# Splitting a weight block's cast from its low part, a second queue for the blocks, and float32r filter taps in a one-core encoder block

## The chip, the cores and the metric

The kernel runs on one core of one Trainium2 chip. The metric is the device time of one execution in microseconds (us). A run consists of several executions of the same program; the profile is one more execution, recorded by the hardware profiler. All tensors are float32 in DRAM.

## The reference, cut to what matters

One encoder block on 512 tokens of width 2048. What matters here is the beginning of it: the modulation, the first projection with the columns of `z_h`, and the filters of the long convolution, which depend on no token at all.

```
mod = silu(c) @ w_ada + b_ada            # c: (1, 2048), w_ada: (2048, 6*2048)
sh1, sc1, g1, sh2, sc2, g2 = split(mod)
h   = x * (1 + sc1) + sh1
z   = h @ w_in + b_in                    # w_in: (2048, 9216)
...
h   = sin(freq * (feats @ w1 + b1)); h = sin(freq * (h @ w2 + b2))
filt = (h @ w3) * window                 # the taps of the filters, then their transforms
...
x   = LN(alpha * x + g1 * mix)           # then an MLP with 2048 -> 8192 -> 2048
```

## The kernel before, in words

Every large product is done in three float32r matmuls, because a float32r operand keeps only part of a float32's digits: an operand `a` is split into a high part (a cast to float32r) and a low part (`a` minus its high part), and `hi*hi + hi*lo + lo*hi` is summed in PSUM. The function `split` (L74) issues the two halves of a splitting together: the cast on ScalarE (L76), the subtraction on VectorE (L77).

Weights come in blocks of 128 by 1024 (512 KB, two row groups of 512 columns). The class `Weights` (L113) keeps a ring of three raw blocks, three high and three low parts. `prepare` takes a loaded raw block, casts it, subtracts, and asks for the next load; all of its loads go out on SyncE's queue (SP). `take` hands the next ready block to a product. Blocks are used in the order of `blocks()`.

The program has four stretches.

**Head.** Small constants are loaded, `cond` (the vector c, the same in all partitions) is turned into silu(c), and the small network of the filters runs: two matmuls with a sine behind each (`Sine`, `Filters.middle`, `Filters.ready`).

**Filters.** Eight parts (n = 0 to 7, in `PARTS`). Each part has taps (four matmuls of the 64 hidden rows with a 512-column piece of w3, in plain float32, L387; every second part has one more for the skip row, L389), the product with a window on VectorE (L397), and a forward transform (`Forward`: six float32 matmuls, L321, L325, L333, and six VectorE sums). One pass of the loop issues the taps of part n+1, the transform of part n, two modulation chunks, the windowed product of part n+1, the stores of the part before, and the sums of part n.

**Value groups.** The modulation's first third (shift1, scale1) is a product of a row with a 2048 by 4096 matrix, and is done on VectorE: 64 chunks of 128 by 1024, each loaded (512 KB) and reduced against `cond` with one instruction (`Modulation.step`, L263). Four chunks give 128 columns of shift and scale; then `first_input` (L424) makes one row group of the activation `h1`: two small sums on GpSimd, two passes on ScalarE (L428, L429), one on GpSimd (L430). Twenty chunks are done during the filters and 44 are left here. Meanwhile two column groups of w_in (4 and 5, the values of the convolution) are computed side by side: `two` holds two generators of `dense_steps`, and each loop pass kp takes one block for each: 24 matmuls (L187) for a block, 16 blocks in all. Before the matmuls of a pass, `prepare` splits as many blocks as the ring holds, and then eight chunks are issued in one go (`ada_steps(4)` twice), so that `h1` is three row groups ahead (`LEAD`). Chunks wait in up to eight buffers of the activation's pool and three of their own, and the next one is asked for when one has been used; nine are on their way at a time while the pool has room. Each row group of `h1` that is finished takes one of these buffers.

**The rest.** All other projections, the convolutions, the branches, the output and the MLP, from the next column group of w_in (6) on.

Each engine runs its instructions in the order in which the code issues them, and so do the two queues' issuers: a DMA that waits holds back every DMA issued behind it on the same engine. Eight semaphores, in turn, serve all DMAs of SP and ScalarE, so that an issue also waits until an earlier DMA, about eight back, has landed.

Of the kernel before, what the change touches and what calls it, by code (L numbers as in the profile page):

```python
# [18 lines left out]
P = 128  # L19
# [21 lines left out]
def block_kernel(ctx: ExitStack, tc: tile.TileContext, t):  # L41
# [70 lines left out]
    class Weights:  # L112


        def __init__(self):
            self.blocks = blocks()
            self.raw, self.ready, self.kept, self.used = [], [], {}, set()
            self.ahead, self.done = 1, False

        def load(self):  # L120
# [5 lines left out]
            load(raw, w[cg, kp])  # L126
# [13 lines left out]
        def prepare(self):  # L140
            for _ in range(4):
# [5 lines left out]
                raw, what = self.raw.pop(0)  # L147
                hi, lo = self.tiles(what)
                split(raw, hi, lo)
                self.ready.append((hi, lo, what))  # L150
                self.load()

        def take(self, w, cg, kp):
            if (w.name, cg, kp) in self.used:
                return self.kept[w.name, cg, kp]
            if not self.done or self.raw:
                self.prepare()
# [67 lines left out]
    cond = const.tile([P, D], F32, name="cond")  # L225
    for h in range(4):
        c_ = slice(512 * h, 512 * (h + 1))
        load(cond[:, c_], t["c"][:, c_].broadcast_to([P, 512]))
# [9 lines left out]
    make_identity(nc, ident)  # L238

# [4 lines left out]
    class Modulation:  # L244
# [16 lines left out]
        def step(self):  # L261
# [3 lines left out]
            if len(self.raw) < 10:  # L265
                self.load()
# [80 lines left out]
    class Filters:  # L347


        def __init__(self):  # L350
            self.one = Sine(hw1, featT, 0, HID)
            self.src, self.raw, self.stores, self.kept, self.win, self.ps = [], [], [], {}, [], []
# [6 lines left out]
        def ready(self):  # L359

            x = self.two.reduce()
            even, odd = slot("a2"), slot("a2")
            nc.scalar.activation(even, x, AF.Sin)
            nc.scalar.activation(odd, x, AF.Sin, scale=sign)
            self.a2 = [a.rearrange("h (p k) -> h k p", k=4) for a in (even, odd)]
# [11 lines left out]

        def taps(self, n):

            cs = PARTS[n][2]  # L380
            if cs == 0:
                self.w = self.raw.pop(0)
            w, skip = self.w
            for cl in range(4):
                ps = bank("flt")
                extra = cs == 0 and cl == 0
                nc.tensor.matmul(ps, self.a2[cs][:, cl, :], w, start=True, stop=not extra)  # L387
# [70 lines left out]
    for s_, c_ in zip(silu, quarters):  # L458
        nc.scalar.activation(s_, c_, AF.Sigmoid)
    flt.middle()  # L460
# [23 lines left out]
    for m in (1, 4):  # L484
        nc.gpsimd.tensor_scalar(bada[:, m], bada[:, m], 1.0, None, op0=OP.add)
    ada_steps(2)
    flt.ready()
    x_load()
# [4 lines left out]
    flt.windowed(0)  # L493
    for n in range(8):
# [666 lines left out]
```

## Time and profile before

| | |
|---|---|
| runs of the kernel before | 2763.06, 2764.24, 2766.48 us (median 2764.24) |
| the profiled execution | 2763.92 us; span of its records 2762.1 us |
| mean granted TensorE clock | 0.993 |
| busy share of the span | TensorE 98%, VectorE 55%, ScalarE 28%, GpSimd 4% |
| bytes read from DRAM, written | 388.01 MB, 10.50 MB |
| head and first taps | 0 to 33.1 us |
| filters (parts 0 to 7) | 33.1 to 98.65 us |
| value groups | 98.65 to 212.6 us |
| the rest | 212.6 to 2762.1 us |

How to read it. PE is TensorE, PEld its weight loads, DVE VectorE, ACT ScalarE, POOL GpSimd, SP SyncE; SPq and ACTq are their DMA issues. Times are counted from the start of the span. The table by windows gives, for each stretch, its length, each engine's busy time with the number of instructions, the granted clock (1.00 is full speed), the mean busy share of the 16 DMA engines and the GB/s that they moved. The timeline gives start, duration, engine, line, operation, tiles, shapes and count, with the idle time before it and what ended that in brackets. A float32 matmul shows as two instructions, a float32r matmul as one. Busy times of neighbours overlap a little, so that the distance of two starts is the better measure of what one costs in a stream.

### The profile page before, as it was taken

To read this page: it belongs to the slowest core of one execution; us is meant where nothing else is said; L and a number is where in the kernel's file an instruction comes from. 1 tells how busy PE (TensorE), PEld (TensorE's weight loads), DVE (VectorE), ACT (ScalarE), POOL (GpSimd) and SP (SyncE) were. 2 spreads that over 40 slices of the span, in tenths; PEclk is the share of its full clock that TensorE was granted. 3 is DMA by queue.
4 is the path that set the end of the run, shared out by engine and by line. 5 is a ranking of instruction groups with operands and counts; after the bars stand their busy time and mean duration, and the time that the engine had idled before them with its cause. 6 is when DMAs were issued, how large, how long until landed. Compare 5 with 4: busy or idle time off the path is not lost.

```text
span 2762.1 us, 29764 instructions
## 1 busy us (share of the span) xinstructions
PE 2703.0 (98%) x11917; PEld 2199.8 (80%) x11917; DVE 1519.6 (55%) x2026; ACT 768.4 (28%) x932; POOL 109.3 (4%) x104
## 2 busy tenths in 40 slices
PE   7989999999999999999999999999999999999996
PEld 3667777888888888887988888888888888888885
DVE  7866968644566657546774343343433433434348
ACT  2234322322222222314631221312213122131232
POOL 1120000000000000050020000000000000000001
PEclk9989999999999999999999999999999999999998
DMA  8672332555665568454552222332222232223242
GB/s 321 241 293 82 127 102 99 190 193 191 201 207 191 185 202 287 139 185 163 167 163 96 99 92 101 98 99 94 97 99 94 97 99 98 94 92 107 93 143 77
DMA packets 120474, 400.46 MB, mean 145 GB/s; under 512 B 14219, under 2 KB 14315, under 8 KB 120208
## 3 DMA queue, kind: packets, MB, share of 16 engines
q1 hardware_dynamic: 119880, 398.20, 42.4%
q8 instruction: 93, 1.52, 0.2%
q10 hardware_dynamic: 456, 0.37, 0.0%
q14 instruction: 45, 0.37, 0.0%
HBM read 388.01 MB, written 10.50 MB: 144 GB/s over the span
## 4 chain that ended last, share of the span: by engine, by line
PE 88%; DVE 4%; DMA 1%; ACT 1%; issue 1%; POOL 0%; SPq 0%; DVEq 0%; ACTq 0%
PE d L187 56%; PE t L874 28%; PE inv L628 1%; DVE wlo L77 1%; PE inv L616 0%; DMA araw<-in_ada 0%; DMA wraw<-in_w_m 0%; DVE r L1026 0%; DVE r L890 0%; PE tr L539 0%; DVE r L1028 0%; PE h2T L914 0%; PE mix L750 0%; PE f L558 0%; PE f L556 0%
## 5 line engine op out<-in xcount | busy, mean ns | idle before, releaser
L187 PE MATMUL d<-act,whi 128*128 128x512 f32 (+1 forms) x4224 | 1285.1, 387 | 15.9 <-POOL act L430 9.0
L77 DVE TENSOR_TENSOR wlo<-wraw,whi 128x1024 fp32r<-128x1024 f32 x480 | 590.3, 1233 | 1030.7 <-ACT whi L76 1027.7
L76 ACT CAST whi<-wraw 128x1024 fp32r<-128x1024 f32 x480 | 504.5, 1054 | 1534.6 <-PE d L187 919.2
L187 PEld LDWEIGHTS d<-act,whi 128*128 128x128 f32 x4224 | 786.7, 189 | 181.3 <-POOL act L430 10.7
L187 PE MATMUL d<-act,wlo 128*128 128x512 f32 (+1 forms) x2112 | 811.9, 384 | 1.8 <-DVE wlo L77 1.8
L187 PEld LDWEIGHTS d<-act,wlo 128*128 128x128 f32 x2112 | 398.5, 189 | 81.7 <-DVE wlo L77 3.5
L874 PE MATMUL t<-whi,fh 128*128 128x512 f32 x960 | 373.4, 389 | 0.0
L874 PE MATMUL t<-wlo,fh 128*128 128x512 f32 x960 | 373.4, 389 | 0.0
L874 PE MATMUL t<-whi,fl 128*128 128x512 f32 x960 | 373.4, 389 | 0.0
L263 DVE SCALAR_TENSOR_TENSOR araw<-araw,cond 128x1024 f32<-128x1024 f32 x192 | 230.3, 1219 | 11.0 <-DMA araw<-in_ada 10.9
L874 PEld LDWEIGHTS t<-whi,fh 128*128 128x128 f32 x960 | 180.2, 188 | 37.5
L874 PEld LDWEIGHTS t<-wlo,fh 128*128 128x128 f32 x960 | 180.2, 188 | 37.4
L874 PEld LDWEIGHTS t<-whi,fl 128*128 128x128 f32 x960 | 180.2, 188 | 37.4
L874 PE MATMUL t<-whi,act 128*128 128x512 f32 x512 | 160.9, 393 | 0.0
L874 PEld LDWEIGHTS t<-whi,act 128*128 128x128 f32 x512 | 96.8, 189 | 20.4
L889 DVE TENSOR_TENSOR gated<-t,cond 128x512 f32<-128x512 f32 x126 | 86.2, 684 | 31.6 <-PE t L874 31.6
L874 PE MATMUL t<-wlo,act 128*128 128x512 f32 x256 | 100.4, 392 | 2.1 <-DVE wlo L77 2.1
L890 DVE TENSOR_TENSOR r<-r,gated 128x512 f32<-128x512 f32 x126 | 87.2, 692 | 4.4
L187 PE MATMUL d<-whi,act 128*128 128x512 f32 x256 | 79.0, 389 | 0.0
L984 DVE TENSOR_TENSOR relu<-relu 128x512 f32<-128x512 f32 (+1 forms) x68 | 45.6, 671 | 38.2 <-ACT fh L983 38.2
L1028 POOL TENSOR_TENSOR r<-r,ln2b 128x512 f32<-128x512 f32 x6 | 10.0, 1662 | 1306.0 <-DVE r L1026 1304.7
L874 PEld LDWEIGHTS t<-wlo,act 128*128 128x128 f32 x256 | 48.5, 189 | 12.3 <-DVE wlo L77 2.5
(220 smaller groups left out, 1886.1 us busy)
## 6 DMA issues: line engine op xcount, KB each, us to landing
wraw<-in_w_m SPq DMA_DIRECT2D x264, 512.0 KB, 3.4
araw<-in_ada SPq DMA_DIRECT2D x192, 512.0 KB, 4.9
wraw<-in_w_in SPq DMA_DIRECT2D x144, 512.0 KB, 3.5
wraw<-in_w_o SPq DMA_DIRECT2D x48, 512.0 KB, 3.9
spec<-spec SPq DMA_DIRECT2D x48, 256.0 KB, 4.0
wraw<-in_w_b SPq DMA_DIRECT2D x16, 512.0 KB, 3.6
wraw<-in_w_a SPq DMA_DIRECT2D x16, 512.0 KB, 3.9
xT<-in_xT SPq DMA_DIRECT2D x16, 256.0 KB, 6.4
```

Source lines behind the costliest of these rows:

```text
L76: nc.scalar.copy(hi, src)
L77: nc.vector.tensor_tensor(lo, src, f32(hi), op=OP.subtract)
L187: nc.tensor.matmul(out[i], a, b, start=first and m == 0, stop=last and m == 2)
L263: nc.vector.scalar_tensor_tensor(raw, raw, 1.0, cond[:, 1024 * h:1024 * (h + 1)], op0=OP.mult, op1=OP.mult, accum_out=dots[:, m, kc, h:h + 1])
L628: nc.tensor.matmul(ps[:, cl * P:(cl + 1) * P], conv.y[cl][cs][:, s], ic(4 * cs + COLUMN[cl]), start=(cs == 0), stop=(cs == 1))
L874: nc.tensor.matmul(out[i], a, b, start=kc == 0 and m == 0, stop=kc == 2 * pairs - 1 and m == 2)
L889: nc.vector.tensor_tensor(x, ps[i], g2_row[c], op=OP.mult)
L890: nc.vector.tensor_tensor(r[i][c], r[i][c], x, op=OP.add)
L984: nc.vector.tensor_tensor(x, x, x, op=OP.mult)
L1028: eng.tensor_tensor(x, x, ln2_b[c], op=OP.add)
```

## The change

**Blocks.** `Weights` gets the halves of a split as two functions: `cast` (ScalarE) and `finish` (VectorE, which then asks for the next load). While the value groups run, a load that `finish` asks for is held in a list and issued by `flush` at the start of the next step, and it goes out on ScalarE's queue instead of SP's. The first three blocks are asked for at n = 2, 3, 4 instead of 4, 5, 6; block 0 is cast at n = 5 and finished at n = 6, block 1 is cast at n = 6.

**Steps.** The eight passes of the value groups become 16 steps u, one block each: flush, then three or four chunks (44 spread over the first 13 steps), then `finish` for block u+1, then the 24 matmuls of block u, then `cast` for block u+2. `take` no longer prepares anything there. After the loop the queue is SP's again.

**Taps.** w3 is split by `Filters.parts` (one split for two parts, issued after the windowed product of the part before), the hidden rows are split in `ready`, and a tap is three float32r matmuls in place of one in float32. The skip row stays float32.

**Head.** The two first small loads go out on SP, ahead of everything; `cond` is loaded in two pieces in place of four and ahead of two others; the two additions of 1 to the bias move from GpSimd to VectorE; `busy(n)` issues n transposes of an identity, whose result nobody reads, before the second sine (10) and before the first taps (28).

**Others.** The stores of a part n = 6 are issued in pass 7. The bound on chunks asked for goes from 10 to 11.

```
         def cast(self):
+            raw, what = self.raw.pop(0)
+            hi, lo = self.tiles(what)
+            nc.scalar.copy(hi, raw)
+            self.half.append((raw, hi, lo, what))
+
+        def finish(self):
+            raw, hi, lo, what = self.half.pop(0)
+            nc.vector.tensor_tensor(lo, raw, f32(hi), op=OP.subtract)
+            self.ready.append((hi, lo, what))
+            self.reload()
...
-    hw1 = cload("hw1", (EMB, HID), nc.scalar)
-    featT = load(slot("featT")[:EMB], t["featT"], nc.scalar)
+    hw1 = cload("hw1", (EMB, HID))
+    featT = load(slot("featT")[:EMB], t["featT"])
...
+    def busy(n):
+        ps = bank("busy")
+        for _ in range(n):
+            nc.tensor.transpose(ps[:, :P], ident, ident)
...
-            nc.scalar.activation(even, x, AF.Sin)
-            nc.scalar.activation(odd, x, AF.Sin, scale=sign)
+            nc.scalar.activation(x, x, AF.Sin)
+            even, odd = slot_pair("a2e"), slot_pair("a2o")
+            split(x, *even)
+            for a, b in zip(even, odd):
+                nc.scalar.activation(b, f32(a), AF.Identity, scale=sign)
...
-                nc.tensor.matmul(ps, self.a2[cs][:, cl, :], w, start=True, stop=not extra)
+                for m, (a, w) in enumerate(((ah, wh), (ah, wl), (al, wh))):
+                    nc.tensor.matmul(ps, a[:, cl, :], w, start=m == 0, stop=m == 2 and not extra)
...
+    weights.later, weights.queue = [], nc.scalar
     for n in range(8):
...
-            flt.store()
+        flt.store()
+        if n < 6:
+            flt.parts(n + 2)
         sums()
-        if 4 <= n < 7:
+        if 2 <= n < 5:
             weights.load()
+        if n == 5:
+            weights.cast()
         if n == 6:
-            weights.prepare()
+            weights.finish()
+            weights.cast()
...
-    for kp in range(8):
-        weights.prepare()
-        while len(h1) < min(KC, 2 * kp + 2 + LEAD):
-            ada_steps(4)
-        for i, group in enumerate(two):
-            next(group)
...
+    first, steps = len(done), 64 - len(done)
+    for u in range(16):
+        kp, i = u // 2, u % 2
+        weights.flush()
+        ada_steps(min(steps, (u + 1) * steps // 13) - len(done) + first)
+        weights.finish()
+        next(two[i])
...
+        weights.cast()
```

How the order changes on three engines. First VectorE, from the last sums of the filters into the value groups. `araw` is a modulation chunk, `wlo` the low part of a block made of `wraw` and its high part `whi`, `spec` a sum of a transform. Before, the numbers being those of the buffers:

```order
L317 TENSOR_TENSOR spec_572<-bf_e0_575,f_o_583 128x512
L77 TENSOR_TENSOR wlo_609<-wraw_503,whi_608 128x1024
L77 TENSOR_TENSOR wlo_615<-wraw_559,whi_614 128x1024
L263 SCALAR_TENSOR_TENSOR araw_372,dots_106<-araw_372,cond_88 128x1024
...
L77 TENSOR_TENSOR wlo_726<-wraw_618,whi_725 128x1024
L263 SCALAR_TENSOR_TENSOR araw_422,dots_106<-araw_422,cond_88 128x1024
...
L263 SCALAR_TENSOR_TENSOR araw_638,dots_106<-araw_638,cond_88 128x1024
L77 TENSOR_TENSOR wlo_796<-wraw_661,whi_795 128x1024
L77 TENSOR_TENSOR wlo_839<-wraw_699,whi_838 128x1024
```

And now, at the same place:

```order
L343 TENSOR_TENSOR spec_701<-bf_e0_704,f_o_712 128x512
L169 TENSOR_TENSOR wlo_680<-wraw_480,whi_679 128x1024
L289 SCALAR_TENSOR_TENSOR araw_456,dots_104<-araw_456,cond_84 128x1024
...
L289 SCALAR_TENSOR_TENSOR araw_591,dots_104<-araw_591,cond_84 128x1024
L169 TENSOR_TENSOR wlo_737<-wraw_548,whi_736 128x1024
L289 SCALAR_TENSOR_TENSOR araw_652,dots_104<-araw_652,cond_84 128x1024
L289 SCALAR_TENSOR_TENSOR araw_655,dots_104<-araw_655,cond_84 128x1024
L289 SCALAR_TENSOR_TENSOR araw_716,dots_104<-araw_716,cond_84 128x1024
L169 TENSOR_TENSOR wlo_821<-wraw_615,whi_820 128x1024
```

Eight chunks and two low parts in turn have become three or four chunks and one low part in turn, and block 1's low part (`wlo_737`) stands behind the chunks of the first step and no longer ahead of the last part's.

Next ScalarE inside the value groups; `act` and `xT` are the two passes that make a row group of h1. The brackets name the semaphores that a row waits for: DMAHW is one of the eight of the DMAs, the others are engines. Before:

```order
L428 ACTIVATE act_745<-xT,mod 128x512 [waits DMAHW7_49,DVE_49,Pool_49]
L429 ACTIVATE xT<-xT,mod 128x512 [waits Activation_49]
L428 ACTIVATE act_765<-xT,mod 128x512 [waits DMAHW0_49,DVE_49,Pool_49]
L429 ACTIVATE xT<-xT,mod 128x512 [waits Activation_49]
L76 CAST whi<-wraw 128x1024 [waits DMAHW1_49,PE_49]
L76 CAST whi<-wraw 128x1024 [waits DMAHW2_49,PE_49]
```

Now, over two steps:

```order
L71 DMA wraw<-in_w_in 128x1024 [waits DMAHW2_49,DVE_49]
L463 ACTIVATE act_884<-xT,mod 128x512 [waits DMAHW4_49,DVE_49,Pool_49]
L464 ACTIVATE xT<-xT,mod 128x512 [waits Activation_49]
L164 CAST whi<-wraw 128x1024 [waits DMAHW5_49,PE_49]
L71 DMA wraw<-in_w_in 128x1024 [waits DMAHW7_49,DVE_49]
L463 ACTIVATE act_943<-xT,mod 128x512 [waits DVE_49,Pool_49]
L464 ACTIVATE xT<-xT,mod 128x512 [waits Activation_49]
L164 CAST whi<-wraw 128x1024 [waits DMAHW2_49,PE_49]
```

One cast follows each row group now, for a block that is used two steps later, and ScalarE issues a block's load, behind a wait for an earlier DMA, ahead of each row group.

Last SP at the end of the filters, where it issues chunks (`araw`), rows of x (`xT`), stores of `spec` and, before, the blocks. Before:

```order
L71 DMA wraw<-in_w_in 128x1024 [waits DMAHW0_49]
L71 DMA araw<-in_ada 128x1024 [waits DMAHW1_49]
L71 DMA araw<-in_ada 128x1024 [waits DMAHW2_49,DVE_49]
L71 DMA wraw<-in_w_in 128x1024 [waits DMAHW3_49]
L71 DMA wraw<-in_w_in 128x1024 [waits DMAHW4_49,DVE_49]
L71 DMA wraw<-in_w_in 128x1024 [waits DMAHW5_49,DMAHW0_49,DVE_49]
L71 DMA araw<-in_ada 128x1024 [waits DMAHW6_49]
```

Now:

```order
L71 DMA araw<-in_ada 128x1024 [waits DMAHW0_49]
L71 DMA araw<-in_ada 128x1024 [waits DMAHW1_49,DVE_49]
L71 DMA araw<-in_ada 128x1024 [waits DMAHW2_49,DVE_49]
L71 DMA araw<-in_ada 128x1024 [waits DMAHW3_49,DVE_49]
L71 DMA xT<-in_xT 128x512 [waits DMAHW4_49,PE_49]
L438 DMA spec<-spec 128x512 [waits DMAHW6_49]
```

No block load, with its wait for a low part on VectorE, stands ahead of a chunk on SP any more.

More of the change, by code (lines that the diff above doesn't have):

```diff
@@ L116, in __init__, with reload, flush @@
             self.blocks = blocks()
-            self.raw, self.ready, self.kept, self.used = [], [], {}, set()
-            self.ahead, self.done = 1, False
+            self.raw, self.half, self.ready, self.kept, self.used = [], [], [], {}, set()
+            self.ahead, self.done, self.later, self.queue = 1, False, None, nc.sync
+        def reload(self):
+            if self.later is None:
+                self.load()
+            else:
+                self.later.append(self.load)
+        def flush(self):
+            while self.later:
+                self.later.pop(0)()
         def load(self):
@@ L125, in load @@
             raw = wts.tile([P, 1024], F32, name="wraw", tag="wraw")
-            load(raw, w[cg, kp])
+            load(raw, w[cg, kp], self.queue)
             self.raw.append((raw, (w.name, cg, kp)))
@@ L146, in prepare, with cast @@
                     return
[L147 to L151, printed above, removed]
+                self.cast()
+                self.finish()
+        def cast(self):
+            raw, what = self.raw.pop(0)
[7 more added lines that the diff above has]
+            self.reload()
         def take(self, w, cg, kp):
@@ L155, in take @@
                 return self.kept[w.name, cg, kp]
-            if not self.done or self.raw:
+            if self.later is None and (not self.done or self.raw):
                 self.prepare()
@@ L376, in fetch, with parts @@
                     self.win.append(load(actp.tile([P, 1024], F32, name="win", tag="act"), t["win"][i]))
+        def parts(self, n):
+            if PARTS[n][2] == 0:
+                w, skip = self.raw.pop(0)
+                both = slot_pair("w3")
+                split(w, *both)
+                self.w.append((*both, skip))
         def taps(self, n):
             cs = PARTS[n][2]
-            if cs == 0:
-                self.w = self.raw.pop(0)
-            w, skip = self.w
+            wh, wl, skip = self.w[0] if cs == 0 else self.w.pop(0)
+            ah, al = self.a2[cs]
             for cl in range(4):
@@ L459, in block_kernel @@
         nc.scalar.activation(s_, c_, AF.Sigmoid)
+    busy(10)
     flt.middle()
@@ L484, in block_kernel @@
     for m in (1, 4):
-        nc.gpsimd.tensor_scalar(bada[:, m], bada[:, m], 1.0, None, op0=OP.add)
+        nc.vector.tensor_scalar(bada[:, m], bada[:, m], 1.0, None, op0=OP.add)
+    busy(14)
     ada_steps(2)
+    flt.parts(0)
     flt.ready()
+    busy(14)
     x_load()
@@ L515, in block_kernel @@
     yv = []
[L516 to L525 removed]
+    first, steps = len(done), 64 - len(done)
[5 more added lines that the diff above has]
+        next(two[i])
+        if kp == 7:
+            next(two[i], None)
+            yv.append(short_conv(ps_v[i], 0, i))
+        weights.cast()
+        if u == 2:
             flt.store()
```

25 lines of the change are left out of this document (11 added, 14 removed).

## The prediction

> **What bounds the kernel now.** I read the page first, then the windows by stage, then the timelines of the stage that has idle time. On the page TensorE is busy for nearly all of the span:
>
> ```profile
> PE 2703.0 (98%) x11917; PEld 2199.8 (80%) x11917; DVE 1519.6 (55%) x2026; ACT 768.4 (28%) x932; POOL 109.3 (4%) x104
> ```
>
> The windows say where the rest is. The columns are the stretch, its length, then PE, PEld, DVE, ACT and POOL busy, the granted clock, the DMA share and GB/s.
>
> ```profile
> 20.50:33.10 12.60, 12.60 (x18) 5.58 (x19) 6.83 (x13) 2.17 (x3) 1.66 (x3) 1.00 1.03 408
> 33.10:98.65 65.55, 65.55 (x152) 33.54 (x150) 60.51 (x97) 11.15 (x16) 4.98 (x9) 1.00 0.63 228
> 85.00:95.00 10.00, 10.00 (x25) 5.39 (x24) 9.43 (x17) 2.52 (x4) 0.00 (x0) 1.00 0.00 0
> 98.65:212.60 113.95, 98.59 (x387) 76.84 (x386) 81.32 (x124) 41.34 (x51) 29.24 (x36) 0.93 0.78 289
> 142.00:158.00 16.00, 13.07 (x52) 10.04 (x51) 11.79 (x19) 5.16 (x7) 5.42 (x7) 0.93 1.03 408
> 140.00:142.00 2.00, 2.00 (x6) 1.58 (x5) 0.34 (x1) 2.00 (x3) 1.23 (x1) 0.50 1.02 418
> 212.60:2762.10 2549.50, 2522.27 (x11362) 2083.04 (x11360) 1358.66 (x1772) 705.97 (x852) 67.03 (x44) 1.00 0.40 134
> ```
>
> The last stretch is TensorE at full clock; nothing in the change reaches into it but the state in which the ring of blocks is handed over, and two blocks stand ready there as before. So the question is the first 212.6 us. In the value groups the 16 blocks need 16 x 24 matmuls, and this piece of the chain of waits gives one at full clock as 21.81 / 96 = 0.227 us:
>
> ```profile
> 254.22 21.81 PE d L187 x96
> ```
>
> So a block is 5.45 us and the stage 87.2 us; it takes 113.95, of which 15.4 is idle (113.95 - 98.59) and about 11 is slow clock (98.59 against 87.2): after a stop the clock is at 0.50 for some microseconds, as in 140 to 142. The stop comes once per pass of two blocks, and the timelines of VectorE and ScalarE show the loop that makes it:
>
> ```profile
> 141.66 2.62 DVE L77 TENSOR_TENSOR wlo<-wraw,whi 128x1024 fp32r<-128x1024 f32 x2 [4.21 <-ACT whi L76]
> 144.19 1.21 DVE L263 SCALAR_TENSOR_TENSOR araw<-araw,cond 128x1024 f32<-128x1024 f32 x1
> ...
> 152.21 1.21 DVE L263 SCALAR_TENSOR_TENSOR araw<-araw,cond 128x1024 f32<-128x1024 f32 x1
> ...
> 157.64 2.61 DVE L77 TENSOR_TENSOR wlo<-wraw,whi 128x1024 fp32r<-128x1024 f32 x2 [4.21 <-ACT whi L76]
> ```
>
> ```profile
> 155.01 0.81 ACT L428 ACTIVATE act<-xT,mod 128x512 fp32r<-128x512 f32 x1 [2.12 <-POOL mod L270]
> 155.86 0.81 ACT L429 ACTIVATE xT<-xT,mod 128x512 f32<-128x512 f32 x1
> 156.58 1.98 ACT L76 CAST whi<-wraw 128x1024 fp32r<-128x1024 f32 x2
> ```
>
> Eight chunks on VectorE (1.145 us from start to start: 144.19 to 152.21 is seven), GpSimd's sums, ScalarE's two passes, then the casts queued behind them, then the low parts on VectorE, which waited 4.21 us: 157.64 - 141.66 = 16.0 us for two blocks, where TensorE needs 10.9.
>
> **The change part by part.** *Cast and low part apart.* The cast of block u+2 now stands a step ahead of its subtraction, so VectorE's 4.21 us of waiting go. Per step VectorE has 44/13 = 3.4 chunks and one low part, 3.4 x 1.145 + 1.25 = 5.1 us, under TensorE's 5.45. If nothing else were late, TensorE would run through. ScalarE gets nothing heavy: per step one cast (0.99), 0.85 of two passes (1.6) and a DMA issue.
>
> *What is late next: the data.* The DMA view of 98.65 to 200 us names what the stage still loads:
>
> ```profile
> q1 hardware_dynamic: 10295, 31.77, 84.6%
> ...
> araw<-in_ada SPq DMA_DIRECT2D x36, 512.0 KB, 8.0
> wraw<-in_w_in SPq DMA_DIRECT2D x13, 512.0 KB, 4.4
> xT<-in_xT SPq DMA_DIRECT2D x10, 256.0 KB, 6.3
> spec<-spec SPq DMA_DIRECT2D x8, 256.0 KB, 4.5
> ```
>
> The four kinds are 30.4 MB (49 of 0.524 and 18 of 0.262). The change removes none of it: I went through the rule for asking for chunks, and in both kernels nine are on their way at the end of the filters and 35 unasked; the raised bound (11 for 10) is never reached, since one chunk used asks for one. What the queue brings is that SP no longer stands still behind blocks:
>
> ```profile
> 73.35 24.66 SPq L71 DMA_DIRECT2D wraw<-in_w_in x3
> ```
>
> Three block issues took 24.66 us there, and from 85 to 95 nothing moved. But the nine buffers were full anyway, so I count nothing for that idle time; only its end moves with VectorE. From the first freed buffer on, 30.4 MB take 74.5 us at the 408 GB/s of a full stretch. They will not all go at that: buffers turn into row groups of h1, so that the chunks on their way fall from nine to five (step 8) and three (step 11). I take 408 for three quarters (55.9 us) and for the last quarter the 314 that the view's 31.86 MB in 101.35 us make (24.2): 80.1 us. The bounds are 74.5 and 96.8, the 314 for all.
>
> The Trainium skill, "DMA: Bandwidth & Descriptors", Specifications, gives about 358 GB/s as what one core gets from its memory; by that the 30.4 MB take 84.9 us. The trace disagrees, with 408 held for 16 us.
>
> *Filters.* TensorE's rows are the taps of parts 5, 6 (with its skip row) and 7 and the start of a transform, VectorE's one pass of the loop and the start of the next:
>
> ```profile
> 66.78 3.60 PE L387 MATMUL flt<-w,a 128*128 128x512 f32 x8
> ...
> 76.31 1.12 PE L389 MATMUL flt<-skip,first_tap 1*128 1x512 f32 x2
> 77.36 2.96 PE L387 MATMUL flt<-w,a 128*128 128x512 f32 x6
> 80.17 1.02 PE L321 MATMUL f_ee<-flt,fwd 128*128 128x512 f32 x2
> ...
> 85.31 3.60 PE L387 MATMUL flt<-w,a 128*128 128x512 f32 x8
> ```
>
> ```profile
> 68.18 1.22 DVE L263 SCALAR_TENSOR_TENSOR araw<-araw,cond 128x1024 f32<-128x1024 f32 x1
> ...
> 70.47 2.48 DVE L397 TENSOR_TENSOR flt<-flt,win 128x512 f32<-128x512 f32 x4
> 72.87 0.67 DVE L337 TENSOR_TENSOR bf_ea<-bf_e,f_eo 128x512 f32<-128x512 f32 x1
> ...
> 76.76 1.22 DVE L263 SCALAR_TENSOR_TENSOR araw<-araw,cond 128x1024 f32<-128x1024 f32 x1
> ```
>
> Two parts take TensorE 85.31 - 66.78 = 18.53 us: two transforms of 5.14 (85.31 - 80.17), a skip row of 1.05 and eight taps of 0.90 ((18.53 - 10.28 - 1.05) / 8). A tap of three float32r matmuls is 3 x 0.227 = 0.68, 1.8 less for two parts. No row shows one with 64 rows; the bounds are that it costs as much as a float32 tap and 0.68, and I take the latter, the price of the same 512 columns. VectorE's pass is 8.4 us (chunks 2.29, products 2.40, sums 3.89 with some 0.2 of waiting), and every second one gets 0.6 for the split of w3, one 128x512 product of that row: 17.4 for two. So VectorE becomes the bound here, and 1.1 of the 1.8 is gained per two parts.
>
> *Head.* The first taps run slowly, and the transform behind them starts at 33.13:
>
> ```profile
> 20.49 2.09 PE L387 MATMUL flt<-w,a 128*128 128x512 f32 x2 [6.07 <-ACT a L363]
> ...
> 24.51 8.79 PE L387 MATMUL flt<-w,a 128*128 128x512 f32 x14
> 33.13 1.02 PE L321 MATMUL f_ee<-flt,fwd 128*128 128x512 f32 x2
> ...
> 223.34 1.12 PE L539 MATMUL tr<-ident,hy 128*128 128x128 f32 x8
> ```
>
> Nine matmuls in 12.6 us where full speed makes 7.7. The 28 transposes cost 0.11 us each at full speed (223.34 to 224.2 is eight), up to twice that slow, 3 to 6 us, and lie in the 6.07 us in which TensorE waits; if that cover were gone they would add as much. I take the taps as fast from 21.0 on (half a microsecond later for the extra cast): 24 x 0.227 and the skip's 1.0 end at 27.4, 5.7 earlier. Little of that reaches the end, since w3's second piece is now needed earlier, for its split in pass 0:
>
> ```profile
> 23.59 0.33 SPq L71 DMA_DIRECT2D w<-in_w  x1
> ...
> DMA to landing us min/median/max: 9.0/9.0/9.0
> ```
>
> It lands at 32.6, in a stretch with the DMA full; with cast and low part (0.6 each) the sums of part 0 start at 33.8. Of these rows the first is their start before, the second that of part 7's chunks:
>
> ```profile
> 35.19 0.67 DVE L337 TENSOR_TENSOR bf_ea<-bf_e,f_eo 128x512 f32<-128x512 f32 x1
> ...
> 97.57 1.22 DVE L263 SCALAR_TENSOR_TENSOR araw<-araw,cond 128x1024 f32<-128x1024 f32 x1
> ```
>
> The gain of the head is 1.4.
>
> *The sum.* VectorE: part 0's sums 33.8 to 37.5, six passes of 8.4, two more splits (1.2) and block 0's low part (1.2): at 90.3 part 7's chunks begin and free the buffers for the loads of the DMA view, at 97.57 before. TensorE starts block 0 about then too, as part 7's transform waits for the last product. Then 80.1 us of data: the last chunk lands at 170.4. Behind it come that chunk and the low part issued behind it (2.3) and three blocks (16.4): 189.0. One spell of slow clock on the path, four microseconds at half, is 2: 191.0. The value groups end there, not at 212.6: 21.6 us less. Against the profiled execution's 2763.92 that is 2742.3, against the median, 0.32 higher, 2742.6.
>
> **The rivals.** *TensorE paces.* If 408 GB/s hold to the end, and loads start some microseconds earlier, the data are in time. Then block 1's low part decides first: it stands behind the two chunks and sums of part 7 and three chunks, 90.3 + 2.3 + 3.7 + 3.4 + 1.2 = 100.9, and 15 blocks and a slow spell of 2 end at 184.7: 28 us less, 2736. For it speaks the full share from 142 to 158, against it the falling number of chunks on their way.
>
> *The second queue brings nothing to the transfers.* If the chunks of one queue and the blocks of the other only take turns, and issues go on waiting for landings about eight back, the data may go at 314 as before: 90.3 + 96.8 + 2.3 + 16.4 + 2 = 207.8, 4.8 us less, 2759. The Trainium skill, "DMA: Bandwidth & Descriptors", section "Issuing engines are not separate DMA queues", says that DMAs of several issuers run on the same 16 engines and that spreading them saves only issue time. By that rule this rival would hold if the queue were what matters; the trace bears it out so far as the share is already 1.03 with one queue, but from 73 to 98 SP lost far more than issue time.
>
> *ScalarE waits for SP's loads (slower).* A block's load now stands on ScalarE ahead of the passes for h1 and the cast, and waits for a DMA about eight back, mostly a chunk's. Where chunks land late, ScalarE stops and all three wait. Unhidden, a block then takes a chunk's landing (8.0), its own (4.4), the cast (1.0) and chunks with low part (5.1), 18.5 us for the two steps that it is ahead: 9.2 a step, 148 in all, an end at 238 and 2790. It is slower than before from (212.6 - 90.3) / 16 = 7.6 us a step on. Against it: h1 is some two to four row groups ahead, and a block's load has its own queue, so 4.4 should fall.
>
> **How the numbers follow.** The data-paced forecast gets 0.63, TensorE's pace 0.20, no gain from the queue 0.10, ScalarE's wait 0.05, and 0.02 that the earlier end is lost again in the handing over of the ring. A measurement of this kernel tells about 0.2%, 5.5 us, from no change. The first two are faster by more; the third, at 4.8, falls about half on either side: 0.89 faster, 0.06 same, 0.05 slower. The range goes from TensorE's pace with 3 us more from the head (2733) to the data at some 330 GB/s and a second slow spell, 92 + 2 us, with an end near 205 (2756).
>
> **What would show it.** Right: the window of the value groups starts near 90 and ends near 191; VectorE's largest wait there is for DMA `araw`, not ACT `whi`; the DMA share is near 1 from 92 to 150; SP has no 24-us stop; the filters' taps take 2.7 us a part. Wrong: PE waits for `wlo` while VectorE waits for ACT (ScalarE's queue decides), an end under 185 (data are no bound), a share under 0.8 with VectorE waiting for `araw` (buffers decide, not the rate), or a first transform still at 33.

## The result, and the profile after

| | before | after |
|---|---|---|
| median, us | 2764.7 (2763.06 to 2766.48) | 2744.43 (2743.02 to 2745.86) |
| profiled execution, us | 2763.92 | 2745.86 |
| head, to the first transform | 33.13 | 28.72 |
| filters, to block 0 on TensorE | 98.65 | 90.58 |
| value groups end | 212.60 | 192.69 |
| first transpose of the rest | 223.34 | 205.96 |

The changed kernel is faster by 0.7%: ratio 0.9928, 95% interval 0.9914 to 0.9942, 20.3 us of medians. The forecast was 2742.6 us. The kernel before has one run more here than in the table of its own above, so that its median is 2764.7 and not 2764.24. Stage by stage, with the stretch, its length, busy PE, PEld, DVE, ACT and POOL, the granted clock, the DMA share and GB/s, the windows of the changed kernel are:

```profile
28.72:90.10 61.38, 61.38 (x173) 36.32 (x172) 59.34 (x100) 13.10 (x19) 5.01 (x9) 1.00 0.76 278
90.10:192.70 102.60, 93.78 (x388) 74.09 (x387) 90.03 (x125) 40.30 (x50) 42.55 (x36) 0.97 0.82 313
95.00:145.00 50.00, 45.81 (x192) 36.56 (x191) 49.56 (x68) 17.29 (x20) 24.81 (x20) 0.97 1.03 401
192.70:205.96 13.26, 11.50 (x50) 8.86 (x48) 10.26 (x12) 6.67 (x9) 0.00 (x0) 1.00 0.34 105
```

Three things are to be seen. VectorE and the DMA are both full from 95 to 145 (49.56 of 50 us, share 1.03), so that the busy shares do not say which of the two is the bound. TensorE still has 8.8 us of idle time in the value groups (102.60 - 93.78), where it had 15.4. And the hand-over to the rest takes 13.26 us, where it took 10.74 (223.34 - 212.60).

What VectorE and TensorE waited for, first in the value groups of the kernel before (the line waited for, us in total, times, longest):

```profile
DVE wlo L77 <- ACT whi L76: 28.3, 8, 4.2
PE d L187 <- POOL act L430: 9.0, 5, 2.0
```

and in those of the changed kernel:

```profile
PE d L207 <- DVE wlo L169: 8.8, 6, 3.8
DVE wlo L169 <- ACT whi L164: 3.4, 2, 3.0
DVE araw L289 <- DMA araw<-in_ada: 2.7, 4, 1.1
```

The 28.3 us in which VectorE waited for a cast are 3.4 now, and 3.0 of those come after the last chunk. TensorE itself waited before mostly for row groups of h1 (`act`), which the chunks on VectorE make: 11.7 of its 15.4 us, 9.0 of them for GpSimd's part. Now all of its 8.8 us are for low parts. But VectorE hardly waits for data either, 2.7 us in all. VectorE simply has more to do than the forecast gave it. Its timeline and GpSimd's, in the middle of the stage, show with what:

```profile
104.11 1.22 DVE L169 TENSOR_TENSOR wlo<-wraw,whi 128x1024 fp32r<-128x1024 f32 x1
105.25 1.21 DVE L289 SCALAR_TENSOR_TENSOR araw<-araw,cond 128x1024 f32<-128x1024 f32 x1
106.02 1.60 POOL L465 TENSOR_TENSOR act<-xT,act 128x512 fp32r<-128x512 f32 x1 [1.78 <-ACT xT L464]
106.39 2.30 DVE L289 SCALAR_TENSOR_TENSOR araw<-araw,cond 128x1024 f32<-128x1024 f32 x1
108.63 1.21 DVE L289 SCALAR_TENSOR_TENSOR araw<-araw,cond 128x1024 f32<-128x1024 f32 x1
108.79 1.11 POOL L295 TENSOR_TENSOR mod<-dots 128x2 f32<-128x2 f32 x1 [1.17 <-DVE araw L289]
...
165.84 1.21 DVE L169 TENSOR_TENSOR wlo<-wraw,whi 128x1024 fp32r<-128x1024 f32 x1
```

A chunk that starts while GpSimd makes the low part of a row group of h1 takes 2.30 us and not 1.22. Of the nine row groups between the low parts at 104.11 and 165.84, seven have such a chunk (2.25 to 2.31 us); in the other two a chunk takes 1.56 us and a low part 1.79. From the one low part to the other are ten steps: 6.17 us for one, where TensorE needs 5.45 and the forecast said 5.1. Of the 1.07 us more, 0.84 are these stretches and 0.2 are waits for chunks and a cast.

### The profile page after: what moved, and what is told of

Same layout as the page of the kernel before. It is cut to its first block, busy times and chain, and to the rows that moved or that the text cites. A ratio compares the mean times of both kernels' runs of the same rounds, so it can differ in the third digit from the quotient of the medians.

```text
span 2744.0 us, 29913 instructions
## 1 busy us (share of the span) xinstructions
PE 2698.5 (98%) x11987; PEld 2208.1 (80%) x11987; DVE 1528.1 (56%) x2033; ACT 772.4 (28%) x938; POOL 117.8 (4%) x102
## 4 chain that ended last, share of the span: by engine, by line
PE 91%; DVE 6%; DMA 1%; issue 1%; ACT 1%; SPq 0%; DVEq 0%; ACTq 0%
PE d L207 57%; PE t L923 29%; DVE araw L289 1%; PE flt L422 1%; DVE wlo L169 1%; PE f_o L359 1%; DMA araw<-in_ada 1%; PE inv L677 1%; PE inv L665 1%; PE f_ee L347 0%; DMA wraw<-in_w_m 0%; PE f_eo L351 0%; DVE r L1075 0%; DVE r L939 0%; PE tr L588 0%
## 5 line engine op out<-in xcount | busy, mean ns | idle before, releaser
L289 DVE SCALAR_TENSOR_TENSOR araw<-araw,cond 128x1024 f32<-128x1024 f32 x192 | 239.8, 1264 | 8.8 <-DMA araw<-in_ada 8.6
L923 PEld LDWEIGHTS t<-whi,act 128*128 128x128 f32 x512 | 97.0, 189 | 20.3
```

Source lines behind the costliest of these rows:

```text
L289: nc.vector.scalar_tensor_tensor(raw, raw, 1.0, cond[:, 1024 * h:1024 * (h + 1)], op0=OP.mult, op1=OP.mult, accum_out=dots[:, m, kc, h:h + 1])
L923: nc.tensor.matmul(out[i], a, b, start=kc == 0 and m == 0, stop=kc == 2 * pairs - 1 and m == 2)
```

## The experiments

All times are medians; "against before" is the difference to the kernel before in the runs beside it (2764.3 to 2764.8). The changed kernel's is -20.3 us; it was not run again beside the experiments, so that a difference to it is a difference of two such differences. The first four ask what paces the value groups now.

**Half the chunk data.** Every second chunk is not loaded; the one before it is reduced a second time in its place.

```
                 m, kc, h = self.order.pop(0)
+                if h and m < 2:
+                    self.raw.append((self.raw[-1][0], self.raw[-1][1], m, kc, h))
+                    return
```

> The changed kernel, in which every second modulation chunk of the first 64 is not loaded: the chunk before it is used again, so that shift1 and scale1 are wrong and 16.8 MB of loads are missing, at the same work on every engine. If the data pace the value groups (theory A), their end moves from 192.7 to about 185, TensorE's pace, and the time falls by 7 to 8 us, to about 2737. If VectorE paces them (theory B: its chunks take 2.3 us in place of 1.2 while GpSimd's subtraction runs beside them), only VectorE's 2.7 us of waits for chunks go: 2741 to 2742.

Measured: 2743.35 us (0.9922, interval 0.9908 to 0.9937), 21.4 less than before. With half of the stage's largest load gone, 1 us is gained, no more than the runs scatter, and less than either theory said. VectorE no longer waits for chunks at all, and its last one still starts at 171.41, where it was 172.66: VectorE's own work takes as long. Data alone are not the bound.

**No GpSimd pass.** The low part of a row group of h1 is written by a pass on ScalarE, which is a copy and not the low part; GpSimd keeps only its small sums.

```
-        nc.gpsimd.tensor_tensor(lo, xt, f32(hi), op=OP.subtract)
+        nc.scalar.activation(lo, xt, AF.Identity)
```

> The changed kernel, in which GpSimd's subtraction for h1's low part is replaced by a pass of the same size on ScalarE (the low part is then wrong). A: data pace, so nothing or under 2 us is gained (2743 to 2745). B: the stretched chunks go, eight or nine times 1.1 us, and the value groups end 6 to 9 us earlier: 2736 to 2738. In both the 2.3-us chunks become 1.2-us ones if it is GpSimd's subtraction that stretches them.

Measured: 2740.94 us (0.9916, interval 0.9901 to 0.993), 23.9 less than before. The groups of VectorE from 92 to 180 us, in the changed kernel (mean ns of one behind the comma, then the idle time ahead of them and what ended it):

```profile
L289 DVE SCALAR_TENSOR_TENSOR araw<-araw,cond 128x1024 f32<-128x1024 f32 x45 | 61.9, 1412 | 2.8 <-DMA araw<-in_ada 2.7
```

and without GpSimd's subtraction:

```profile
L289 DVE SCALAR_TENSOR_TENSOR araw<-araw,cond 128x1024 f32<-128x1024 f32 x45 | 53.9, 1223 | 9.8 <-DMA araw<-in_ada 9.6
```

The chunks are 8.0 us cheaper in all, so the stretch is GpSimd's doing. But 7 of the 8 us turn into waits for chunks: now the data pace, as the forecast had it, and the last chunk starts at 171.31, in the changed kernel at 172.66. The time lies between those of the two theories.

```profile
171.31 1.23 DVE L289 SCALAR_TENSOR_TENSOR araw<-araw,cond 128x1024 f32<-128x1024 f32 x1 [0.51 <-DMA araw<-in_ada]
```

**Both.** The two edits together.

> Both edits together: half the chunk data, and no subtraction on GpSimd (shift1, scale1 and h1's low part are wrong). Neither data nor the stretch are left, so that block 1's low part and TensorE's pace decide: an end near 184.7, 2736 to 2737, by both theories. A: no better than the run with half the data alone. B: no better than the run without GpSimd's subtraction alone. If it beats both by 2 us or more, data and VectorE bind by turns.

Measured: 2736.72 us (0.99, interval 0.9885 to 0.9915), 28.1 less than before and 7.7 less than the changed kernel, where the two alone brought 1.1 and 3.5. Two bounds stand at the same height: take away one and the other holds. What TensorE still waits for in the value groups with both gone is almost all the low part of block 1, at the place where the forecast's first rival had it:

```profile
102.01 0.50 PE L207 MATMUL d<-act,wlo 128*128 128x512 f32 x1 [3.45 <-DVE wlo L169]
```

**The low part of h1 on VectorE.** The same line with `nc.vector`, nothing left out.

> The changed kernel with h1's low part subtracted on VectorE in place of GpSimd; nothing is left out. VectorE gets 12 subtractions of about 0.6 us in the value groups and loses the stretch of about 1.1 us each. B: 0.4 to 0.5 us a row group, 4 to 6 us less, 2739 to 2740. A: nothing, 2743 to 2745; it may also cost up to 3 us, since a subtraction on VectorE waits there for ScalarE's two passes and holds back the chunks queued behind it.

Measured: 2780.54 us (1.0058, interval 1.0042 to 1.0075), 15.7 more than before: a miss. No chunk is stretched, but VectorE now stands behind ScalarE's pass in each row group, and TensorE behind VectorE:

```profile
DVE act L465 <- ACT xT L464: 22.8, 10, 2.3
PE d L207 <- DVE wlo L169: 19.0, 9, 7.8
```

That is the wait that the change removed, put back with another tile: an instruction of VectorE issued right behind the ScalarE pass that it needs. The whole gain goes, and more.

The next four undo one part of the change each.

**One queue.** The blocks load from SyncE's queue, as before.

```
-    weights.later, weights.queue = [], nc.scalar
+    weights.later, weights.queue = [], nc.sync
```

> The block loads of the value groups go out on SyncE's queue again, all else as in the changed kernel (2744.4 us). If the second queue is what freed SyncE from standing behind blocks (theory one), issues of chunks wait behind issues of blocks again, the DMA share from 95 to 155 us falls below 0.95, VectorE waits more for araw than the 2.7 us of the changed kernel, and the time is 2748 to 2756 us. If the queue brings nothing, since both queues feed the same 16 engines and a load that is asked for a step later finds its buffer free anyway (theory two), the time stays within 2 us of 2744.4 and the share at 1.03. A stop of SyncE of over 20 us between 70 and 95 us would cost nothing by either, because the buffers are full then.

Measured: 2743.55 us (0.9926, interval 0.9913 to 0.9938). Theory two: the queue brings nothing that these runs can tell. A window of this run holds the same rate:

```profile
125.00:155.00 30.00, 29.21 (x124) 22.67 (x124) 29.53 (x42) 12.71 (x16) 15.48 (x12) 1.00 1.03 407
```

The rule that DMAs of several issuers share the same 16 engines (the Trainium skill, "DMA: Bandwidth & Descriptors", section "Issuing engines are not separate DMA queues") agrees: share 1.03 with one queue and with two. SyncE's long stop is there with either (26.31 us with one queue); here is the changed kernel's, whose four issues are chunks that wait for a buffer:

```profile
66.73 26.10 SPq L71 DMA_DIRECT2D araw<-in_ada  x4
```

**Float32 taps.** One float32 matmul for a tap; w3 and the hidden rows are not split.

```
...
-                both = slot_pair("w3")
-                split(w, *both)
-                self.w.append((*both, skip))
+                self.w.append((w, w, skip))
...
-                for m, (a, w) in enumerate(((ah, wh), (ah, wl), (al, wh))):
-                    nc.tensor.matmul(ps, a[:, cl, :], w, start=m == 0, stop=m == 2 and not extra)
+                nc.tensor.matmul(ps, ah[:, cl, :], wh, start=True, stop=not extra)
```

> The taps are one float32 matmul again, w3 and the hidden rows are not split, all else as in the changed kernel. If VectorE paces the filters in the changed kernel (theory one, the step of the prediction: 1.8 us less on TensorE for two parts, but 0.6 us more on VectorE), TensorE paces again at about 18.5 us for two parts against 17.4, block 0 starts some 3 us later, near 93.5, and the time is 2746 to 2749 us. If the taps bring nothing, because the split costs VectorE what TensorE saves (theory two), block 0 starts within 1 us of 90.6 and the time stays at 2743 to 2745.5.

Measured: 2744.75 us (0.9929, interval 0.9915 to 0.9943). Block 0 starts on TensorE where theory one had it, and the time is theory two's. The sums of part 0, part 7's first chunk and block 0, in this run:

```profile
29.00 0.68 DVE L363 TENSOR_TENSOR bf_ea<-bf_e,f_eo 128x512 f32<-128x512 f32 x1
...
90.96 1.22 DVE L289 SCALAR_TENSOR_TENSOR araw<-araw,cond 128x1024 f32<-128x1024 f32 x1
...
93.17 1.02 PE L207 MATMUL d<-act,whi 128*128 128x512 f32 x2
```

and in the changed kernel:

```profile
33.03 0.69 DVE L77 TENSOR_TENSOR w3l<-w,w3h 128x512 fp32r<-128x512 f32 x1 [1.73 <-ACT w3h L76]
33.64 0.68 DVE L363 TENSOR_TENSOR bf_ea<-bf_e,f_eo 128x512 f32<-128x512 f32 x1
...
90.10 1.22 DVE L289 SCALAR_TENSOR_TENSOR araw<-araw,cond 128x1024 f32<-128x1024 f32 x1
...
90.58 1.03 PE L207 MATMUL d<-act,whi 128*128 128x512 f32 x2
```

The split taps win on TensorE what the forecast counted, but their split of w3's second piece holds up the first sums by 4.6 us (33.64 - 29.00). Over the filters they get that back and 0.9 us more on VectorE. TensorE's own 2.6 us (93.17 - 90.58) are worth nothing, since it then waits for VectorE's next low part: 3.76 us in the changed kernel, 2.01 here.

**No idle transposes.** The three calls of `busy` are taken out.

```
-    busy(10)
...
-    busy(14)
...
-    busy(14)
```

> The transposes that nobody reads are left out (38 of them), all else as in the changed kernel. If they only keep the clock up and the sums of part 0 wait for w3's second piece anyway (theory one, the step of the prediction), the first taps run at a granted clock of about 0.5, the first transform starts some 4 to 6 us later than 28.7, the sums of part 0 at most 2 us later than 33.7, and the time is 2744 to 2747 us. If the clock in the head decides the time (theory two), it is 2748 to 2751 us. If they stand in the way of the taps (theory three), it is 2741 to 2743 us.

Measured: 2744.58 us (0.9927, interval 0.9915 to 0.994). The first transform starts 2.1 us later, at 30.86, and the sums of part 0 at 33.67, as before the edit (33.64): theory one, with no measurable cost. That it is 2.1 us and not the 4 to 6 expected comes in part from the changed kernel's side: there too TensorE waits 2.23 us between the last transpose and the first tap, and the granted clock is 0.50 from 23.10 to 25.70. Where no split stands in the way, in the float32 run, the taps behind the transposes ran at 1.00 and the first transform started at 26.94, so what the transposes are worth is shown here only for the change as it is.

```profile
30.86 1.02 PE L347 MATMUL f_ee<-flt,fwd 128*128 128x512 f32 x2
...
33.67 0.68 DVE L363 TENSOR_TENSOR bf_ea<-bf_e,f_eo 128x512 f32<-128x512 f32 x1
```

**Cast and low part together, chunks spread.** In each step the cast of block u+1 stands right ahead of its low part.

```
         ada_steps(min(steps, (u + 1) * steps // 13) - len(done) + first)
+        if u:
+            weights.cast()
         weights.finish()
...
-        weights.cast()
...
+    weights.cast()
     weights.finish()
```

> In each step of the value groups the cast of block u+1 is issued right ahead of its low part, behind the step's chunks and row group, and no longer a step before; one block a step, chunks spread and ScalarE's queue as in the changed kernel. If the distance between cast and low part is what removed VectorE's wait (theory one), VectorE waits for ScalarE's cast in each step, as it did for 4.21 us in each pass before, a step takes 7 us or more, and the time is 2752 to 2770 us. If the spreading of the chunks alone removed it, because ScalarE is free when the cast is issued (theory two), VectorE's waits for whi stay under 10 us in all and the time is within 3 us of 2744.4.

Measured: 2770.05 us (1.002, interval 1.0011 to 1.0029), 5.7 more than before: theory one, at the end of its range. The waits in its value groups:

```profile
DVE wlo L169 <- ACT whi L164: 34.6, 13, 3.2
PE d L207 <- ACT whi L164: 15.1, 7, 4.8
```

VectorE waits for a cast again, 2.7 us a time, and spreading the chunks makes it worse than before: thirteen waits in place of eight.

**Apart, chunks in bunches.** The other half: the cast stays a step ahead, but eight chunks are issued in one go ahead of every second block, as before.

```
-        ada_steps(min(steps, (u + 1) * steps // 13) - len(done) + first)
+        while i == 0 and len(h1) < min(KC, 2 * kp + 5):
+            ada_steps(4)
```

> The chunks are issued as in the kernel before, eight ahead of every second block (four blocks apart in h1's lead), all else as in the changed kernel: the cast stays a step ahead of its low part. If the distance between cast and low part carries the gain alone (theory one), VectorE still never waits for ScalarE's casts and the time is within 4 us of 2744.4. If the spreading is needed as well (theory two), each pair's first low part stands behind eight chunks, TensorE waits about 5 us once in two blocks, its clock falls behind each stop, and the time is 2752 to 2762 us.

Measured: 2755.58 us (0.9966, interval 0.9954 to 0.9978), 9.3 less than before: theory two. One pass on VectorE and ScalarE shows why:

```profile
111.97 1.99 ACT L164 CAST whi<-wraw 128x1024 fp32r<-128x1024 f32 x2
113.04 1.49 DVE L169 TENSOR_TENSOR wlo<-wraw,whi 128x1024 fp32r<-128x1024 f32 x1 [3.00 <-ACT whi L164]
114.45 1.21 DVE L289 SCALAR_TENSOR_TENSOR araw<-araw,cond 128x1024 f32<-128x1024 f32 x1
...
123.61 2.27 DVE L169 TENSOR_TENSOR wlo<-wraw,whi 128x1024 fp32r<-128x1024 f32 x1
```

Where the chunks are bunched, the odd step has none, so the second low part of a pair follows the first at once and meets a cast that is still queued behind ScalarE's passes: a step apart in the program is no time apart on VectorE. The rest is the stop behind eight chunks (TensorE waits 18.0 us for `wlo`, 6 times). The 9.3 us are not the value groups' either. From block 0 on TensorE to the first transpose of the rest this run takes 124.8 us, and the kernel before 124.7 (223.34 - 98.65):

```profile
91.85 1.02 PE L207 MATMUL d<-act,whi 128*128 128x512 f32 x2
...
216.66 1.12 PE L589 MATMUL tr<-ident,hy 128*128 128x128 f32 x8
```

The last three try to go further; nothing is left out of them.

**One block further ahead.** Block 1 is finished ahead of part 7's chunks and sums, a step finishes block u+2 and casts block u+3.

```
+        if n == 7:
+            weights.finish()
+            weights.cast()
         ada_steps(2)
...
-        weights.finish()
+        if u < 15:
+            weights.finish()
         next(two[i])
+        if u < 14:
+            weights.cast()
...
-        weights.cast()
...
-    weights.finish()
```

> The ring works one block further ahead: block 1's low part stands ahead of part 7's chunks and sums on VectorE, and a step finishes block u+2 and casts block u+3, ahead of the convolution behind the last blocks. Nothing is left out. If VectorE's pass of chunks and low parts paces the whole stage (theory one), the wait of 3.8 us for block 1 and the slow clock behind it were not on the path, the last chunk still ends near 173.8, one block less stands behind it, and the two low parts at the hand-over no longer wait: 3 to 7 us less, 2738 to 2741 us. If TensorE's waits in the stage are what counts (theory two), another 5 us go: 2733 to 2736 us. If the earlier low parts push the chunks back on VectorE by more than that (theory three), it stays within 2 us of 2744.4.

Measured: 2740.83 us (2739.68 to 2742.5; 0.9914, interval 0.99 to 0.9927), 24.0 less than before: the best version that leaves nothing out, and its runs lie below all of the changed kernel's, though the two intervals overlap. The early wait is gone, and TensorE is busy without a stop from 95 to 125. The time is theory one's, its reason only in part: the last chunk comes later (176.51 for 172.66, where theory one left it in its place), but one block less stands behind it:

```profile
95.00:125.00 30.00, 30.00 (x134) 24.86 (x133) 30.00 (x43) 9.91 (x12) 13.74 (x11) 1.00 1.00 381
```

One thing was expected and did not come: at the hand-over TensorE still waits for a low part behind the convolution's sums, once and 1.63 us long in place of twice.

```profile
198.08 0.50 PE L207 MATMUL d<-act,wlo 128*128 128x512 f32 x1 [1.63 <-DVE wlo L169]
```

**The low part of h1 on VectorE, two chunks later.**

```
...
+    def low_part(eng):
+        hi, lo, x = low.pop(0)
+        eng.tensor_tensor(lo, x, f32(hi), op=OP.subtract)
         h1.append((hi, lo))
...
                 x_load()
+            if len(done) % 4 == 2 and low:
+                low_part(nc.vector)
```

> In the value groups the low part of a row group of h1 is made on VectorE, as in the run that came out slower, but two chunks later than ScalarE's passes, so that VectorE should not wait for them; during the filters it stays on GpSimd. Nothing is left out. If a chunk's stretch beside GpSimd's subtraction is what lifts VectorE's step from 5.1 to 6.2 us (theory one), no chunk takes over 1.25 us, VectorE pays 0.69 in place of 1.08 us for a row group, the waits for ScalarE's pass are gone, and the time is 2739 to 2743 us. If the data pace anyway (theory two), VectorE's waits for araw grow by what it saves and the time stays within 2 us of 2744.4. If the deferred low part makes h1 late (theory three), TensorE waits for act and it is 2748 us or more.

Measured: 2751.23 us (0.9948, interval 0.9935 to 0.996), 13.6 less than before and so 6.7 slower than the changed kernel: a miss. VectorE waits again, 12.4 us in ten waits:

```profile
101.94 1.11 POOL L295 TENSOR_TENSOR mod<-dots 128x2 f32<-128x2 f32 x1 [5.87 <-DVE araw L289]
...
103.13 1.07 POOL L296 TENSOR_TENSOR mod<-mod,c_bada 128x2 f32<-128x2 f32 x1
...
104.24 0.81 ACT L463 ACTIVATE act<-xT,mod 128x512 fp32r<-128x512 f32 x1 [8.60 <-POOL mod L296]
105.09 0.82 ACT L464 ACTIVATE xT<-xT,mod 128x512 f32<-128x512 f32 x1
...
105.94 0.69 DVE L473 TENSOR_TENSOR act<-xT,act 128x512 fp32r<-128x512 f32 x1 [1.78 <-ACT xT L464]
```

Two chunks (2.3 us) are shorter than what they should cover: two sums on GpSimd that last as long as the chunks beside them, and two passes of 0.82. The time is theory three's, but what TensorE waits for is VectorE's low parts of blocks, not h1.

**Both of these.**

> The two before this one together; nothing is left out. If they act on different parts, the path behind the last chunk and VectorE's pace, their gains add up: 2734 to 2740 us, with TensorE's pace (2736) as the floor. If both are limited by the data, it comes out like the first of them alone, within 2 us.

Measured: 2746.86 us (0.9935, interval 0.9923 to 0.9948), 18.0 less than before. The gain of the first (3.7) and the loss of the second (6.7) nearly add up, to 2.3 more than the changed kernel, in neither of the ways expected.

## Why the prediction was right, and which steps were not

**The head: right.** The sums of part 0 were to start at 33.8, behind the split of w3's second piece, and start at 33.64. That the taps end at 28.72 and not at 27.4 costs nothing for the same reason, and neither do the transposes bring anything here.

**The filters: right in the sum, one-sided in the parts.** Part 7's chunks were to start at 90.3 and start at 90.10. The forecast booked 1.1 us gained per two parts for the taps and, in another place, the wait for w3 in the head, without saying that one edit makes both. The float32 run puts them against each other: 0.9 us are left. The mark of 2.7 us for a part's taps was missed: part 7's take 3.2, from 77.47 to 80.69.

**VectorE's step: wrong, the mis-sized term.** "3.4 x 1.145 + 1.25 = 5.1 us, under TensorE's 5.45" was worked out from chunks of the kernel before, where GpSimd's subtractions fell into VectorE's 4.21 us of waiting (at 152.97, as the last of eight chunks ended, and at 156.75). With the wait gone they fall beside chunks. A step is 6.17 us, above TensorE's 5.45, and where GpSimd's pass is taken out the chunks are back at 1.22. The forecast's sum had no term for this, so that VectorE, which was to stay under TensorE's pace, runs above it.

**The data: the size right, its part only half.** Its last chunk was to land at 170.4. With the stretches gone it is the data that VectorE waits for (9.6 us, 13 times), and the last chunk starts at 171.31. In the changed kernel VectorE's own work takes as long (171.41 with half the data gone), and the last chunk starts at 172.66. That the forecast of the time held is in part luck, for these two paces happen to be alike: the mark that it set itself, VectorE's largest wait for `araw`, was not met (2.7 us against 3.4 for `whi`, and 6.2 for the convolution at the end).

**The second queue: right to count nothing for it, wrong about the mark.** SyncE stops for 26.10 us still. The rival named after it had its premise confirmed and its consequence refuted: with one queue the data go at 378 GB/s from 90.3 to 170 and not at the 314 that it took. That this is because VectorE now asks for them without a stop is argued: it fits its 29.53 busy us of 30 in the window above, but no run shows it by itself.

**The hand-over: wrong.** That "two blocks stand ready there as before" does not hold. In the changed order the low parts of the next blocks stand behind the convolution's sums on VectorE, and TensorE waits twice:

```profile
193.87 0.50 PE L207 MATMUL d<-act,wlo 128*128 128x512 f32 x1 [0.57 <-DVE wlo L169]
...
200.79 0.50 PE L207 MATMUL d<-act,wlo 128*128 128x512 f32 x1 [1.19 <-DVE wlo L169]
```

The value groups end at 192.69 (forecast 191.0), 1.7 us late, and the hand-over takes 13.26 us for 10.74, of which these two waits are 1.76. The rest of the kernel behind it takes 0.7 us less than in the profile before (2538.04 for 2538.76). Together this is 3.5 of the 3.6 us between the profiled execution's forecast of 2742.3 and its 2745.86.

**The other rivals.** TensorE's pace was priced at 2736; with data and GpSimd out of the way the kernel takes 2736.72. Its early sign, block 1's low part at 100.9, came in the changed kernel too, with the spell of slow clock that the sum had in it:

```profile
100.00:105.00 5.00, 4.19 (x11) 3.35 (x12) 5.00 (x8) 0.73 (x1) 2.18 (x2) 0.66 1.04 422
...
100.81 0.50 PE L207 MATMUL d<-act,wlo 128*128 128x512 f32 x1 [3.76 <-DVE wlo L169]
```

ScalarE's wait for its own loads stayed small: its casts waited 1.3 us in all for `wraw`.

**Which part of the change carries the gain.** Against before: apart and spread -20.3, apart and bunched -9.3, together and spread +5.7, together and bunched (the kernel before) 0. The kernel before is not a clean fourth corner, since it has the old head and filters too: its block 0 starts at 98.65, that of the other three at 90.58, 91.85 and 90.77. So each of the three is 7 to 8 us ahead when the value groups begin. From there to the first transpose of the rest the four take 115.4 us (apart and spread), 124.8 (apart and bunched), 139.7 (together and spread, to 230.42) and 124.7 (before). In these profiles neither half brings anything alone in the value groups: casting ahead needs the spreading, and spreading without casting ahead costs 15 us. Queue, taps and transposes, each undone alone, move nothing that these runs tell from zero, so what brings the 8.1 us ahead of block 0 stays open in part. With float32 taps the sums of part 0 start at 29.00, where they started at 35.19 before, so that the head's other edits together can make most of it. The loads' order at the start, the bound of 11 and the earlier first blocks were not tried by themselves.

## What to carry to other kernels

Issuing the two halves of a pass further apart pays only if real work of the waiting engine lies between them: check what that engine does in between, not how many steps apart the halves are issued. When a wait is removed, list what another engine used to do inside it, and price that work again beside the work that now fills the time. And when two resources come out full in the same windows, take each away alone and then both, since either run alone shows little of what both give together.

## What the runs showed of the hardware

GpSimd and VectorE hold each other up, one instruction at a time, and by these rows it depends on where their operands lie (they are different instructions; no run moves an operand alone). In the value groups a chunk reads two tiles of SBUF: beside GpSimd's 128x512 subtraction it takes 2.30 us for 1.22, and GpSimd's own take 1.60 for 1.28 and, for a sum of 128x2, 1.11 for 0.20. In the filters the same subtraction runs beside VectorE sums that read one tile of SBUF and one of TensorE's results, and there nobody waits:

```profile
42.04 0.67 DVE L363 TENSOR_TENSOR bf_ea<-bf_e,f_eo 128x512 f32<-128x512 f32 x1
42.05 1.27 POOL L465 TENSOR_TENSOR act<-xT,act 128x512 fp32r<-128x512 f32 x1 [1.77 <-ACT xT L464]
42.74 0.69 DVE L341 SCALAR_TENSOR_TENSOR bf_e<-bf_e,f_eo 128x512 f32<-128x512 f32 x1
```

This is the rule of the Trainium skill, "SBUF — State Buffer", section "Who interferes with whom": a VectorE instruction with two SBUF inputs contends with a GpSimd instruction that reads SBUF, and the later one blocks until the other is done. The rows agree: GpSimd's pass from 106.02 ends at 107.62, and the chunk started at 106.39 ends 1.07 us behind that, at 108.69, close to the 1.22 of a chunk alone. The trace of the kernel before showed the sign: the same sum of GpSimd, beside VectorE's chunks and in VectorE's wait.

```profile
148.93 1.11 POOL L269 TENSOR_TENSOR mod<-dots 128x2 f32<-128x2 f32 x1 [6.88 <-DVE araw L263]
...
154.51 0.19 POOL L269 TENSOR_TENSOR mod<-dots 128x2 f32<-128x2 f32 x1
```

The clock can fall after a wait that is short. In the run with blocks further ahead TensorE stood for 2.21 us, and the clock granted behind that was about half for some 3.4 us, until 154.8; a wait of 1.87 us at 161.08 in the changed kernel, and one of 2.01 at 101.68 in the float32 run, left it at 1.00. The Trainium skill, "TensorE: Matmul & The Clock Gate", section "What's actually happening", gives an idle window of about 3.4 us as what brings half the rate; here less did. Whether it is the length of a wait or where it falls that decides, these runs do not show. The wait, and the windows behind it:

```profile
151.09 0.56 PE L207 MATMUL d<-act,wlo 128*128 128x512 f32 x1 [2.21 <-DVE wlo L169]
```

```profile
151.00:153.00 2.00, 1.91 (x5) 1.58 (x6) 1.49 (x5) 0.00 (x0) 0.00 (x0) 0.60 1.01 405
153.00:155.00 2.00, 2.00 (x6) 1.55 (x6) 1.76 (x3) 0.00 (x0) 0.49 (x1) 0.55 1.05 411
```
